# Two products of a chunk's result, issued head by head in turn over column halves, in the delta net and in the gated mixer

## The chip, the cores and the metric

The kernel runs on one core of a Trainium2 chip. The metric is the device time of one execution in microseconds (us). The engines are TensorE (PE in the profile, its weight loads PEld), VectorE (DVE), ScalarE (ACT), GpSimd (POOL) and SyncE (SP), which here only issues DMAs.

## The reference, cut to what matters

One inference step of a two-layer decoder over 512 prompt tokens and 8 samples of 4 tokens. Each layer splits one input projection among four mixers; then come an output projection, a layer norm and a channel mixer (a dense SwiGLU in the first layer, 8 experts in the second). Two of the four mixers are touched here: the gated delta net (4 heads of width 64) and HGRN2, the gated mixer (4 heads of width 64). Per chunk and head they compute:

```python
# delta net, one chunk of one head
o = einsum('ck,kv->cv', q * exp(gcum), S) + einsum('ij,jv->iv', einsum('ik,jk->ij', q, k) * decay, v_new)
S = S * exp(glast) + einsum('ck,cv->kv', k * exp(glast - gcum), v_new)
# gated mixer, one chunk of one head
o = einsum('ik,kv->iv', q * exp(b), S) + einsum('ij,jv->iv', att, v)
S = exp(blast) * S + einsum('jk,jv->kv', k * exp(blast - b), v)
```

Either result is a sum of products that go into one accumulation.

## The kernel before

The residual stream lies transposed in SBUF (features over 128 partitions, tokens along the free axis). The large products (projections, channel mixer, experts) run as three products of split operands each (`xh`, `xl` with `wh`, `wl`) on weights streamed from HBM. The small products of the mixers are float32; every float32 product is two matmul instructions in the trace, each with its own weight load.

**Work around the change.** In `mixers`, in each of the two layers, `b_chunks` works on the prompt in 4 chunks of 128 tokens with two pairs of heads, `i` = 0 and 1. A pair lies on the 128 partitions, head `h` on the half `hs(h)` (0 to 63 or 64 to 127). The chunk loop is a recurrence: the state `st` (tile `gst`) of a chunk is needed by the next. Per chunk it forms `vn` (tile `wk`), the state's new part (`kt` with `vn`), and then for each pair the result in the PSUM tile `op_` (tile `mx`): `vn` with `pt` (read from the trace as `mx<-pt,wk`) for every chunk, and from the second chunk on `st` with `q` (read as `mx<-arr,gst`), accumulated into the same columns. The first product contracts over 128 partitions into 64 result partitions (128*64 in the trace), the second over 64 into 64 (64*64), with head 0 and head 1 in opposite halves of the array's rows and of its columns. When both heads of a pair have theirs, VectorE updates the state (L1026); after both pairs ScalarE copies the result out (L1029). After the last chunk GpSimd issues the store of the state (L1030).

`mix_c` is a generator over two pairs and 4 chunks of 128 tokens. A chunk's result, in `op_` (columns 256 to 383 of `p2`, tile `mx`), is the state's product (`mx<-qec,hst`), then for each head the values `kt[:, 1]` (tile `ktc`) with `offd` and with `diag`, both 128*64. `offd` is written by ScalarE (L1197, L1200), `diag` by GpSimd. Behind them come the products for the state's update (`mx<-ktc`).

**What sets the order.** All instructions are handed to a scheduler that orders each engine's queue by a simulated timeline and fills an engine's waits with other ready work: in the trace the chunks of the delta net stand among the products of the differential attention (tiles `dx`, `pg`, `kv`), which reads its paged keys and values from HBM through SP's queue (L641), and the chunks of the gated mixer stand among its own next products (`kq`), the input projections (`st`) and the attention's last. `mm` (L292) records nearly every matmul, so groups are told apart by tiles.

Of the kernel before, what the change touches and what calls it, by code (L numbers as in the profile page):

```python
# [267 lines left out]
def _body(ctx, tc, I, O):  # L268
# [22 lines left out]
    def mm(out, lhsT, rhs, start=True, stop=True):  # L291
        return PE.matmul(out, lhsT, rhs, start=start, stop=stop)  # L292
# [192 lines left out]
    def mixers(l, y32, hook):  # L485
# [352 lines left out]
        def hs(h):  # L838
            return slice(64 * (h % 2), 64 * (h % 2) + 64)

        def b_chunks(bp, k, q, v, gt_, be, beh, kde, bge):
            def wk(w=512):
                return bp.tile([128, 512], F32, name="wk", bufs=3)[:, 0:w]
# [3 lines left out]
            kt = bp.tile([128, 2, 4, 128], F32, name="kt", bufs=1)  # L847
            erl = bp.tile([128, 2, 4], F32, name="erl", bufs=1)
            for i in range(2):
                hh = slice(2 * i, 2 * i + 2)  # L850
                for cp2 in range(2):
# [29 lines left out]
                    for u in range(2):  # L881
                        c = 2 * cp2 + u
# [111 lines left out]
            for c in range(4):  # L994
                tok = slice(128 * c, 128 * c + 128)
                vc = v[:, :, tok]
                if c > 0:
                    t1 = wk(256)
                    for h in range(2):
                        ks = mx()  # L1000
                        for i in range(2):
                            mm(ks[:, 64 * i:64 * i + 64], k[hs(h), i, tok], st[hs(h), i])
                        tt(V, t1.rearrange("p (i h d) -> p h i d", i=2, h=2)[:, h], ks[:, 0:128].rearrange("p (i d) -> p i d", i=2),
                           bc(bge[:, c].rearrange("p (i h) -> p h i", h=2)[:, h], 64), OP.mult)
                    tt(V, vc, vc, t1.rearrange("p (i d) -> p i d", i=2), OP.subtract)
                vp_ = mx()
                for i in range(2):
                    for h in range(2):
                        o = 128 * i + 64 * h
                        mm(vp_[:, o:o + 64], lt[:, 8 * i + 2 * c + h], vc[:, i, 64 * h:64 * h + 64])  # L1010
                vn = wk(256)
                S.activation(vn, vp_[:, 0:256], AF.Copy)
                op_ = mx()
                for i in range(2):
                    for h in range(2):
                        o = 128 * i + 64 * h
                        mm(op_[hs(h), 256 + 64 * i:320 + 64 * i], kt[:, i, c, 64 * h:64 * h + 64], vn[:, o:o + 64])
                for i in range(2):
                    src = op_[:, 256 + 64 * i:320 + 64 * i]
                    for h in range(2):  # L1020
                        o = 128 * i + 64 * h
                        mm(op_[hs(h), 128 * i:128 * i + 128], vn[:, o:o + 64], pt[:, 8 * i + 2 * c + h], start=True, stop=c == 0)
                        if c > 0:
                            mm(op_[hs(h), 128 * i:128 * i + 128], st[hs(h), i], q[hs(h), i, tok], start=False, stop=True)
                    if c > 0:
                        V.scalar_tensor_tensor(st[:, i], st[:, i], erl[:, i, c:c + 1], src, op0=OP.mult, op1=OP.add)  # L1026
                if c == 0:
                    V.tensor_copy(st, op_[:, 256:384].rearrange("p (i d) -> p i d", i=2))
                S.activation(v[:, :, tok], op_[:, 0:256].rearrange("p (i t) -> p i t", i=2), AF.Copy)  # L1029
# [111 lines left out]
        def mix_c(bp, sp, kk, b, q, iv):  # L1141
            oc = iv
            diag = [bp.tile([128, 2, 128], F32, name="diag%d" % a, bufs=1) for a in range(2)]
            offd = [bp.tile([128, 2, 128], F32, name="offd%d" % a, bufs=1) for a in range(2)]
# [24 lines left out]
            for i in range(2):  # L1169
                st = bp.tile([128, 128], F32, name="hst", bufs=2)  # L1170
                G.memset(st, 0.0)
                for c in range(4):
                    c0 = TOKS[c][0]
                    if c % 2 == 0:
                        kq = {s: level(s, i, c0, 256) for s in (64, 32, 16, 8, 4, 2, 1)}
                        if c:
                            yield
                    k0 = 128 * (c % 2)
                    tok = slice(c0, c0 + 128)
                    p1 = [mx() for _ in range(2)]  # L1180
                    p2 = mx()
                    for h in range(2):
                        spr = p1[h][:, 0:192].rearrange("p (g i) -> p g i", g=6)
                        mm(p1[h][0:64, 192:256], kq[64][hs(h), k0:k0 + 64], kq[64][hs(h), k0 + 64:k0 + 128])
                        for u in range(2):
                            mm(p1[h][64 * u:64 * u + 32, 256:288], kq[32][hs(h), k0 + 64 * u:k0 + 64 * u + 32],
                               kq[32][hs(h), k0 + 64 * u + 32:k0 + 64 * u + 64])
                        for j, s in enumerate((16, 8, 4, 2, 1, 0)):
                            for u in range(4):
                                sl = slice(32 * u, 32 * u + 32)  # L1190
                                ksl = slice(k0 + 32 * u, k0 + 32 * u + 32)
                                tsl = slice(c0 + 32 * u, c0 + 32 * u + 32)
                                if s:
                                    mm(spr[sl, j], kq[s][hs(h), ksl], kq[s][hs(h), ksl])
                                else:
                                    mm(spr[sl, j], kk[hs(h), i, tsl], q[hs(h), i, tsl])
                        S.activation(offd[c % 2][0:64, h, 64:128], p1[h][0:64, 192:256], AF.Copy)  # L1197
                        for u in range(2):
                            sl = slice(64 * u, 64 * u + 32)
                            S.activation(offd[c % 2][sl, h, 64 * u + 32:64 * u + 64], p1[h][sl, 256:288], AF.Copy)  # L1200
                        smx = bp.tile([128, 6, 32], F32, name="smx", bufs=2)
                        tt(V, smx, spr, C("hmask").rearrange("p (g i) -> p g i", g=6), OP.mult)
                        sml = bp.tile([128, 32], F32, name="sml", bufs=2)
                        V.tensor_reduce(sml, smx.rearrange("p g i -> p i g"), axis=AX.X, op=OP.add)
                        tt(G, diag[c % 2][:, h].rearrange("p (u i) -> p u i", u=4), mid(sml, 4), bc(C("quad"), 32), OP.mult)
                    eb = bp.tile([128, 128], F32, name="eb", bufs=2)
                    S.activation(eb, b[:, i, tok], AF.Exp)
                    kd = bp.tile([128, 128], F32, name="kdc", bufs=KDB)
                    S.activation(kd, b[:, i, tok], AF.Exp, scale=-1.0, bias=b[:, i, c0 + 127:c0 + 128])
                    tt(V, kd, kd, kk[:, i, tok], OP.mult)  # L1210
                    qe = bp.tile([128, 128], F32, name="qec", bufs=KDB)
                    tt(V, qe, q[:, i, tok], eb, OP.mult)
                    PE.transpose(p2[:, 0:128], kd, ident)
                    PE.transpose(p2[:, 128:256], iv[:, i, tok], ident)
                    kt = bp.tile([128, 2, 128], F32, name="ktc", bufs=KDB)
                    S.activation(kt, r2(p2[:, 0:256]), AF.Copy)
                    op_ = p2[:, 256:384]
                    mm(op_, st, qe, start=True, stop=False)
                    for h in range(2):
                        vs = slice(64 * h, 64 * h + 64)  # L1220
                        mm(op_[hs(h)], kt[:, 1, vs], offd[c % 2][:, h], start=False, stop=False)
                        mm(op_[hs(h)], kt[:, 1, vs], diag[c % 2][:, h], start=False, stop=True)
                    for h in range(2):
                        vs = slice(64 * h, 64 * h + 64)
                        mm(p2[hs(h), 384:448], kt[:, 0, vs], kt[:, 1, vs])
                    S.activation(oc[:, i, tok], op_, AF.Copy)
                    for h in range(2):
                        sd = st[hs(h), 64 * h:64 * h + 64]
                        V.scalar_tensor_tensor(sd, sd, eb[hs(h), 127:128], p2[hs(h), 384:448], op0=OP.mult, op1=OP.add)
                for h in range(2):  # L1230
                    G.dma_start(O["hp"][l, hs(h), i], st[hs(h), 64 * h:64 * h + 64])
                yield
# [36 lines left out]
            for i in range(2):  # L1269
                op_ = mx()  # L1270
                for h in (2 * i, 2 * i + 1):
                    mm(op_[hs(h), 0:32], vk[32 * h:32 * h + 32, 0], ats[32 * h:32 * h + 32], start=True, stop=False)
                for bb in range(NB):
                    for h in (2 * i, 2 * i + 1):
                        mm(op_[hs(h), 4 * bb:4 * bb + 4], s0[i][hs(h), bb, :], ebs[hs(h), 2, i, 4 * bb:4 * bb + 4],
                           start=False, stop=bb == NB - 1)
                V.tensor_copy(oc[:, i, sm], op_[:, 0:32])
            for i in range(2):
                sp_ = mx()
                for h2 in range(2):  # L1280
                    h = 2 * i + h2
# [918 lines left out]
```

## Time and profile before

| what | value |
|---|---|
| median of 3 timed runs | 2100.49 us (2093.48 to 2102.44) |
| profiled execution, its own time | 2082.73 us |
| its span in the trace | 2081.1 us |
| TensorE matmul busy | 1949.0 us (94%), 17620 instructions |
| VectorE busy | 1296.1 us (62%) |
| ScalarE busy | 946.4 us (45%) |
| GpSimd busy | 369.5 us (18%) |
| mean granted TensorE clock | 0.96 |

The durations come from the profiled execution. Its time lies 17.76 us under the median of the timed runs. Matmuls are pipelined and their ends are modelled, so the distance between the starts of two matmuls tells more than their durations.

### The profile page before, as it was taken

How to read it: one execution, taken by the hardware profiler on the slowest of the kernel's cores; microseconds unless marked ns; L12 is line 12 of the kernel's file. 1: busy time of each engine (PE TensorE's matmuls, PEld its weight loads, DVE VectorE, ACT ScalarE, POOL GpSimd, SP SyncE). 2: the span in 40 equal slices, each digit the busy share in tenths (PEclk: the TensorE clock that was granted, in tenths of full speed). 3: DMA queues.
4: the chain of work that ended last, by engine and by line, in shares of the span. 5: the costliest groups of instructions: out<-in, count | busy, mean ns of one | idle time of the engine just before them, and what ended most of it. 6: DMA issues, size and time to landing. Idle time of an engine off the chain costs nothing. (4 is left out here: it accounts for less than half of the span.)

```text
span 2081.1 us, 46801 instructions
## 1 busy us (share of the span) xinstructions
PE 1949.0 (94%) x17620; PEld 1755.5 (84%) x17620; DVE 1296.1 (62%) x2597; ACT 946.4 (45%) x1833; POOL 369.5 (18%) x542
## 2 busy tenths in 40 slices
PE   8999989998999999989999989995999999999985
PEld 7877747887999999978787648894999999999985
DVE  4566556766333333653566566666887877777786
ACT  3445234644322223442544234643666665556532
POOL 1220022202000000031120033100220303404350
PEclk9999998989999999999999999996999999999998
DMA  6557451332222332545554543134879868787961
GB/s 240 153 155 187 138 170 57 97 117 87 83 85 79 101 92 74 153 137 176 173 147 139 170 129 101 54 123 171 262 233 325 292 227 280 234 270 248 332 198 66
DMA packets 183924, 340.93 MB, mean 164 GB/s; under 512 B 28035, under 2 KB 103912, under 8 KB 183688
## 3 DMA queue, kind: packets, MB, share of 16 engines
q1 hardware_dynamic: 160744, 287.67, 43.4%
q0 software_dynamic: 13968, 48.04, 7.4%
q10 hardware_dynamic: 8976, 2.13, 0.5%
q8 instruction: 141, 2.31, 0.5%
q14 instruction: 95, 0.78, 0.1%
HBM read 319.91 MB, written 17.85 MB: 162 GB/s over the span
## 5 line engine op out<-in xcount | busy, mean ns | idle before, releaser
L295 DVE TENSOR_TENSOR wl<-wraw,wh 128x1024 fp32r<-128x1024 f32 (+2 forms) x474 | 550.5, 1164 | 337.0 <-ACT wh L376 331.1
L376 ACT ACTIVATE wh<-wraw 128x1024 fp32r<-128x1024 f32 (+2 forms) x474 | 463.2, 980 | 478.4 <-PE st L292 258.9
L292 PE MATMUL st<-xh,wh 128*128 128x256 f32 (+1 forms) x1536 | 461.8, 301 | 20.1 <-ACT wh L376 8.1
L292 PE MATMUL st<-xh,wl 128*128 128x256 f32 (+1 forms) x1536 | 456.8, 298 | 3.8 <-DVE wl L295 3.6
L292 PE MATMUL st<-xl,wh 128*128 128x256 f32 (+1 forms) x1536 | 456.1, 297 | 4.3 <-DVE xl L295 4.3
L292 PEld LDWEIGHTS st<-xh,wh 128*128 128x128 f32 x1536 | 299.4, 195 | 38.8 <-issue 8.8
L292 PEld LDWEIGHTS st<-xh,wl 128*128 128x128 f32 x1536 | 299.3, 195 | 16.5 <-issue 10.4
L292 PEld LDWEIGHTS st<-xl,wh 128*128 128x128 f32 x1536 | 299.6, 195 | 10.9 <-DVE xl L295 5.2
L292 PE MATMUL st<-xg,wh 128*128 128x416 f32 (+4 forms) x880 | 240.0, 353 | 2.6 <-DVE m_g L1766 1.5
L292 PE MATMUL st<-xg,wl 128*128 128x208 f32 (+4 forms) x880 | 212.4, 242 | 0.0
L292 PEld LDWEIGHTS st<-xg,wh 128*128 128x128 f32 x880 | 166.4, 189 | 4.6 <-issue 2.7
L292 PEld LDWEIGHTS st<-xg,wl 128*128 128x128 f32 x880 | 169.0, 192 | 0.0
L292 PE MATMUL st<-hg,wh 128*128 128x416 f32 (+4 forms) x440 | 123.9, 358 | 0.2 <-ACT wh L376 0.2
L1495 POOL TENSOR_SCALAR r<-r,par 128x256 f32<-128x256 f32 (+1 forms) x32 | 30.6, 969 | 449.8 <-ACT xh L1494 449.8
L292 PE MATMUL st<-hg,wl 128*128 128x208 f32 (+4 forms) x440 | 108.5, 248 | 1.9 <-DVE wl L295 1.9
L292 PE MATMUL st<-wh,xg 128*128 128x256 f32 x528 | 105.6, 293 | 4.2 <-DVE xg L1753 4.2
L295 POOL TENSOR_TENSOR m_g<-m_g,m_u 128x208 f32<-128x208 f32 (+4 forms) x55 | 52.7, 958 | 307.7 <-DVE m_u L1766 272.4
L292 PE MATMUL ff<-hh,wl 128*128 128x256 f32 (+1 forms) x352 | 101.8, 292 | 4.9 <-DVE wl L295 4.9
L292 PE MATMUL ff<-hh,wh 128*128 128x256 f32 (+1 forms) x352 | 101.8, 290 | 1.5 <-ACT wh L376 1.5
L292 PE MATMUL ff<-xh,wh 128*128 128x256 f32 (+1 forms) x352 | 102.4, 291 | 0.5 <-ACT wh L376 0.5
L292 PE MATMUL ff<-xl,wh 128*128 128x256 f32 (+1 forms) x352 | 102.2, 291 | 0.0
L292 PE MATMUL ff<-xh,wl 128*128 128x256 f32 (+1 forms) x352 | 102.0, 290 | 0.0
(583 smaller groups left out, 3851.4 us busy)
## 6 DMA issues: line engine op xcount, KB each, us to landing
pg<-in_kc_dram SPq DMA_DIRECT2D x256, 128.0 KB, 2.7
pg<-in_vc_dram SPq DMA_DIRECT2D x256, 128.0 KB, 2.5
wraw<-in_w_in_dram POOLq DMA_DIRECT2D x56, 512.0 KB, 4.4
wraw<-in_m_g_dram SPq DMA_DIRECT2D x54, 512.0 KB, 4.9
wraw<-in_m_u_dram SPq DMA_DIRECT2D x54, 512.0 KB, 4.9
wraw<-in_m_g_dram SPq DMA_DIRECT2D x65, 256.0 KB, 5.1
wraw<-in_m_u_dram SPq DMA_DIRECT2D x65, 256.0 KB, 5.7
wraw<-in_w_o_dram SPq DMA_DIRECT2D x32, 512.0 KB, 3.8
```

Of the source, the lines that this page charges most:

```text
L292: return PE.matmul(out, lhsT, rhs, start=start, stop=stop)
L295: return e.tensor_tensor(out, a, b, op=op)
L376: S.activation(h, r, AF.Copy)
L1495: G.tensor_scalar(ri[:, u], ri[:, u], gcol[:, u:u + 1], bcol[:, u:u + 1], op0=OP.mult, op1=OP.add)
```

## The change

The four products of a pair's result are issued in another order. In the delta net: `vn` with `pt` for head 0, for head 1, then `st` with `q` for head 0, for head 1 (before: both of head 0, then both of head 1). In the gated mixer: `offd` for head 0, for head 1, then `diag` for head 0, for head 1. The number of instructions, their operands, the flags that begin an accumulation and the tiles are the same; the flag that ends one stands on the last product of each head as before.

```diff
                     for h in range(2):
                         o = 128 * i + 64 * h
                         mm(op_[hs(h), 128 * i:128 * i + 128], vn[:, o:o + 64], pt[:, 8 * i + 2 * c + h], start=True, stop=c == 0)
-                        if c > 0:
+                    if c > 0:
+                        for h in range(2):
                             mm(op_[hs(h), 128 * i:128 * i + 128], st[hs(h), i], q[hs(h), i, tok], start=False, stop=True)
                     if c > 0:
                         V.scalar_tensor_tensor(st[:, i], st[:, i], erl[:, i, c:c + 1], src, op0=OP.mult, op1=OP.add)
...
                     mm(op_, st, qe, start=True, stop=False)
-                    for h in range(2):
-                        vs = slice(64 * h, 64 * h + 64)
-                        mm(op_[hs(h)], kt[:, 1, vs], offd[c % 2][:, h], start=False, stop=False)
-                        mm(op_[hs(h)], kt[:, 1, vs], diag[c % 2][:, h], start=False, stop=True)
+                    for j, a in enumerate((offd, diag)):
+                        for h in range(2):
+                            mm(op_[hs(h)], kt[:, 1, 64 * h:64 * h + 64], a[c % 2][:, h], start=False, stop=j == 1)
```

## Rows read from the trace of the kernel before

**Rows 1.** The page: busy time, then PE and its granted clock in 40 slices.
```profile
PE 1949.0 (94%) x17620; PEld 1755.5 (84%) x17620; DVE 1296.1 (62%) x2597; ACT 946.4 (45%) x1833; POOL 369.5 (18%) x542
...
PE   8999989998999999989999989995999999999985
...
PEclk9999998989999999999999999996999999999998
```

**Rows 2.** Busy time of each engine by stretch; PEclk is the mean granted clock.
```profile
core 0: us, PE busy (x) PEld busy (x) DVE busy (x) ACT busy (x) POOL busy (x), PEclk, DMA share, GB/s
240.00:440.00 200.00, 186.23 (x2250) 136.19 (x2249) 126.02 (x339) 93.25 (x255) 46.70 (x107) 0.91 0.39 113
440.00:960.00 520.00, 496.56 (x3801) 486.31 (x3801) 230.06 (x352) 171.68 (x271) 37.38 (x44) 0.99 0.35 106
```

**Rows 3.** Timeline of PE, second chunk of the delta net, first layer.
```profile
262.01 0.38 PE L292 MATMUL mx<-pt,wk 128*64 128x128 f32 x2
262.32 0.43 PE L292 MATMUL mx<-arr,gst 64*64 64x128 f32 x2
262.68 0.43 PE L292 MATMUL mx<-pt,wk 128*64 128x128 f32 x2
263.05 0.43 PE L292 MATMUL mx<-arr,gst 64*64 64x128 f32 x2
263.85 0.43 PE L292 MATMUL mx<-pt,wk 128*64 128x128 f32 x2 [0.38 <-DVE gst L1026]
264.21 0.43 PE L292 MATMUL mx<-arr,gst 64*64 64x128 f32 x2
264.57 0.43 PE L292 MATMUL mx<-pt,wk 128*64 128x128 f32 x2
264.93 0.43 PE L292 MATMUL mx<-arr,gst 64*64 64x128 f32 x2
265.29 0.44 PE L292 MATMUL mx<-gst,arr 64*128 64x64 f32 x4
```

**Rows 4.** All instructions that touch the tile gst, the state's product and its update.
```profile
L292 PE MATMUL mx<-arr,gst x48: 269/320/472, 262.3 to 1212.7; 64*64 64x128 f32 x48
L1026 DVE SCALAR_TENSOR_TENSOR gst<-gst,erl,mx x12: 279/280/282, 263.5 to 1213.1; 128x64 f32<-128x64 f32 x12
```

**Rows 5.** Timeline of PE, one array half's products in a row, one after another.
```profile
326.32 1.09 PE L292 MATMUL dx<-kv,vt 128*64 128x128 f32 x8
327.34 0.69 PE L292 MATMUL dx<-arr,y 32*128 32x512 f32 x1
```

**Rows 6.** Timeline of PE, first chunk of the delta net: no state's product.
```profile
254.50 0.61 PE L292 MATMUL mx<-pt,wk 128*64 128x128 f32 x8
255.04 0.44 PE L741 MATMUL dx<-cst,kv 128*128 128x128 f32 x2
```

**Rows 7.** Timeline of PE, the sample part of the gated mixer.
```profile
419.17 1.10 PE L292 MATMUL mx<-ebs,s2k 64*64 64x4 f32 x32
420.20 0.30 PE L292 MATMUL mx<-ats,vk 32*64 32x32 f32 x4
```

**Rows 8.** Timeline of PE, mixer chunk with nothing between its products; the last such.
```profile
360.69 0.45 PE L292 MATMUL mx<-offd,ktc 128*64 128x128 f32 x4
360.96 0.40 PE L292 MATMUL mx<-diag,ktc 128*64 128x128 f32 x4
361.18 0.29 PE L292 MATMUL mx<-ktc 128*64 128x64 f32 x4
361.40 0.39 PE L292 MATMUL st<-xh,wh 128*128 128x256 f32 x1
...
1334.13 0.45 PE L292 MATMUL mx<-offd,ktc 128*64 128x128 f32 x4
```

**Rows 9.** Timeline of PE, mixer chunk with other work between its products.
```profile
372.65 0.43 PE L292 MATMUL mx<-offd,ktc 128*64 128x128 f32 x2
373.02 0.24 PE L292 MATMUL mx<-kq 64*32 64x32 f32 x2
373.19 0.32 PE L292 MATMUL mx<-diag,ktc 128*64 128x128 f32 x1
...
373.56 0.25 PE L292 MATMUL mx<-kq 64*32 64x32 f32 x2
373.74 0.32 PE L292 MATMUL mx<-diag,ktc 128*64 128x128 f32 x1
...
374.21 0.38 PE L292 MATMUL mx<-kq 64*32 64x32 f32 x22
```

**Rows 10.** What PE waited for, 250 to 290 us: us in total, times, longest.
```profile
PE dx L292 <- DMA pg<-in_vc_dram: 0.9, 1, 0.9
```

**Rows 11.** Timeline of all engines at the end of the delta net.
```profile
288.86 0.55 POOL L1030 DMA_DIRECT2D out_gp_dram<-gst  x1 [36.40 <-DVE gst L1026]
...
295.48 0.64 PE L292 MATMUL dx<-pg,kv 128*32 128x256 f32 x8 [2.06 <-DMA pg<-in_vc_dram]
```

**Rows 12.** Busy time by stretch of 10 us, columns as in Rows 2.
```profile
260.00:270.00 10.00, 8.77 (x80) 5.00 (x80) 3.70 (x11) 3.60 (x9) 0.00 (x0) 1.00 0.40 112
...
290.00:300.00 10.00, 6.20 (x86) 3.28 (x86) 7.24 (x31) 5.83 (x18) 5.44 (x17) 1.00 0.56 166
300.00:310.00 10.00, 7.39 (x36) 2.87 (x40) 9.28 (x38) 3.38 (x9) 7.49 (x20) 0.92 0.81 238
310.00:320.00 10.00, 8.86 (x48) 6.07 (x41) 6.45 (x21) 4.74 (x13) 4.37 (x13) 0.57 0.41 122
320.00:420.00 100.00, 100.00 (x1607) 83.57 (x1608) 69.88 (x177) 57.71 (x169) 27.21 (x54) 0.95 0.27 75
```

## The prediction

> **What bounds the kernel now.** I read the page first. TensorE is busy 94% of the span and no slice of the mixers falls out of that [rows 1], so an instruction that leaves TensorE's time should be worth nearly its length, if it sits where TensorE is the last to end. The table by stretch says the same for the stage that the change touches: 186.23 of 200 us in the first layer's mixers, and 496.56 of 520 in the dense channel mixer behind them [rows 2]. Then I went to the timeline of TensorE inside one chunk. The four products of a pair of heads, two matmuls each, start 0.36 us apart (262.32, 262.68, 263.05; again from 263.85 on), small as they are [rows 3]. That spacing, and not the durations printed beside it, is the price of a product here.
>
> **Why 0.36 us.** Compare two other places. Eight matmuls of one array half and one shape, 128*64, take 327.34 - 326.32 = 1.02 us until the next shape starts [rows 5]. With p for a matmul and e for the change of shape, 8p + e = 1.02, and for a product between two changes 2p + e = 0.36 [rows 3]. So p = 0.11 and e = 0.14 us: each of the four products pays a change of shape, from 128*64 to 64*64 and back. In the first chunk, which has no state's product, four products with eight matmuls take 255.04 - 254.50 = 0.54 us [rows 6]. One after another they would take 1.02; as two column halves side by side 4p + e = 0.58. So head 0 and head 1 of the 128*64 product do run beside each other when nothing of another shape stands between.
>
> **The change, part by part: delta net.** Nothing is added or removed: the same matmuls, no DMA, no copy. The order of a pair becomes 128*64 twice, then 64*64 twice. The first two run beside each other by [rows 6]. For the second two I need a row of 64*64 products in opposite halves of rows and columns that go to one PSUM tile. The sample part of the gated mixer has it: 32 matmuls in 420.20 - 419.17 = 1.03 us, change of shape included, that is (1.03 - 0.14)/16 = 0.056 us for two of them [rows 7]. They are short (4 columns), so the row shows that both halves accept work together, and bounds nothing about 128 columns. I take the pair as side by side, 2p + e = 0.36, because the nearest row with 128 columns, [rows 6], overlaps fully; the other end, one behind the other, is 4p + e = 0.58.
>
> A pair of heads then costs 2 x 0.36 = 0.72 instead of 4 x 0.36 = 1.44 us. The very first product of a chunk comes in its own shape (262.01 to 262.32, 0.31 us) before and after, so the saving is the same. The update L1026 runs 12 times [rows 4], once for each pair of the second to fourth chunk in both layers, so there are 12 such groups (48 matmuls with the state's product are 12 x 2 heads x 2). The sum is 12 x 0.72 = 8.6 us; at the other end 12 x (1.44 - 2 x 0.58) = 12 x 0.28 = 3.4 us, if in both shapes the second product stands behind the first.
>
> The Trainium skill speaks against this edit: TensorEngine Tiling (Array Packing), section Restrictions and Gotchas, Gotcha 1, says that different row tiles cannot use one PSUM bank at once, and head 0 and head 1 of the state's product are such row tiles in one bank. By that rule the 64*64 pair would stay serial and the sum would be 12 x 0.50 = 6.0 us. The 0.056 us for two matmuls in [rows 7] do not look like it.
>
> What waits behind these products? L1026 needs both heads' products, since it overwrites the state. It now starts 0.72 us earlier, and the next pair, which stood 0.38 us for it [rows 3], follows. Head 0's state product moves behind head 1's first product, which reads a tile that is already there; no wait is added.
>
> **Gated mixer.** Both products have one shape, so there is no change of shape to save inside. Of the 16 chunks, 7 run as in the first group of [rows 8], to the last at 1334.13: four products from 360.69 to 361.18, 0.49 us, which is 4p plus little. That is already side by side, whatever order they were issued in, so the edit gives nothing there. In the other 9 other work stands between, as in [rows 9]: 374.21 - 372.65 = 1.56 us against 361.40 - 360.69 = 0.71 up to the same point; without the two visits (0.17 and 0.18) 1.21, so 0.50 us of overlap and changes of shape are lost. If all 9 lost nothing, that is 4.5 us. But what is put between stands between `offd` and `diag`, and the new order keeps that border, only with both heads on either side. I take 0.6 us, near to nothing. The other end: if the new border lets work in between the 7 whole ones, 7 x 0.50 = 3.5 us are lost. A late `offd` of head 1 would now hold up `diag` of head 0 and all that TensorE has queued behind it; the trace of the waits shows none for either tile.
>
> **What of it arrives.** 9.2 us leave TensorE. In the stretch around the delta net it is busy for 93% [rows 2], so I count 0.93 x 9.2 = 8.5 us. The rest of the stage hangs on the delta net's end too: GpSimd stands 36.40 us at the store of the state until the last L1026, with its later work behind it [rows 11], so those chains come forward with TensorE. Against the profiled execution: 2082.73 - 8.5 = 2074.2. The timed runs lie above it (median 2100.49), so I carry over the difference: 2100.5 - 8.5 = **2092 us**, 0.4% less. A measurement of this kernel tells about 0.5%, 10.5 us, from no change; the forecast falls inside that.
>
> **Rivals.**
>
> *The mixer gains too* (0.22). The 9 broken chunks close up, because the scheduler sees an independent product behind each: 8.6 + 4.5 = 13.1, times 0.93 gives 12.2 us, 2088. For it: half of the border's products now have a neighbour that is ready. Against it: where the work is put in, it was put in at the same border. The Trainium skill has a rule by which the mixer would gain otherwise: TensorE: Matmul & The Clock Gate, Part 3, says that matmuls start and end strictly in program order. Head 0's two products would then have been serial everywhere, and one slot of 0.22 us would go in each of 16 chunks, 3.5 us, so 2089. The 0.49 us of [rows 8] bear it out only if the scheduler had already put the products in the new order.
>
> *The second product stands behind the first* (0.08): 3.4 x 0.93 = 3.2 us, 2097. [rows 6] speak against it for one half of the gain, [rows 7] for the other.
>
> *The time is absorbed* (0.13). TensorE only reaches its waits for key and value pages sooner: 0.9 us at one wait before the delta net's end [rows 10], 2.06 us behind it [rows 11], and 290 to 320 us holds 7.6 us of idle time [rows 12]. If pages come no earlier, 4.3 us per layer vanish there: 2100, no change. Against it: SP's page loads wait for TensorE to free their buffers, so they move forward with it, and from 320 to 420 us TensorE is busy all of 100 us [rows 12].
>
> *Slower: idle TensorE drops its clock* (0.07). Where TensorE idled, at 290 to 310 us (13.59 of 20 us busy), the next 10 us were granted 0.57 of the clock, close to 1.2 GHz [rows 12]; at that level a 10 us stretch does the work of 5.7. If shorter chunks put more idle time there and the low level lasts longer, each 10 us cost 4.3. From 20 us more in the two layers together the gain is gone, from 44 us on the kernel is slower by over 0.5%; with 60 us more, 26 - 8.5 = 17.5 us, 2118. Against it: 260 to 270 us was also idle for 1.2 us and stayed at 1.00 [rows 12].
>
> **Chances and range.** The forecast has 0.50. Its own terms run from 6 us (one shape serial) to 11 us, so a part of it, about 0.13, lies beyond 10.5 us; of the mixer's rival at 12.2 about 0.19. Faster by over 0.5%: 0.32. Slower: 0.07 and a little for an order of the scheduler that costs in the mixer (3.5 us) and elsewhere, 0.08. Within: 0.60. The range reaches to 2083 (the mixer's rival, less the 4.5 us by which the timed runs spread) and to 2103 (time absorbed, plus 2 to 3 us of that spread); below lies some 0.1, above some 0.1.
>
> **What will show it.** In the profile after, in each of 12 groups: `pt` of both heads starting within some hundredths of a us, `gst` of both heads 0.36 us later, the next instruction another 0.36 us later. If the `gst` pair takes 0.58, one shape is serial. In the mixer: four `offd` matmuls together, four `diag`, and nothing or one visit between. If the groups shrink and the span does not, the waits for `pg` between 290 and 330 us must have grown. The prediction is wrong if the scheduler lays the stage out anew, which would show in the order of the work around these groups, not in them.

## The result, and the profile after

| | before | after |
|---|---|---|
| median | 2093.48 us (2082.57 to 2110.67, 20 runs) | 2076.74 us (2069.26 to 2088.54, 20 runs) |
| ratio | | 0.9927, 95% interval [0.9910, 0.9945] |
| profiled execution | 2082.73 us | 2087.53 us |

The kernel is faster by 0.73%, 15.3 us (11.5 to 18.8). The median of before is lower here than the 2100.49 us of its first three runs, which are among these twenty and lie from their middle upwards. The two profiled executions mislead if they are set side by side: that of before is one of the fastest of its kernel, that of after one of the slowest of its own. So these two spans are not compared below, but groups of instructions and stages, over several kernels.

The page of after, which answers to [rows 1] (busy time; PE and its granted clock in 40 slices): TensorE is as busy as before and nearly the whole of the span.

```profile
PE 1947.4 (93%) x17620; PEld 1754.9 (84%) x17620; DVE 1296.5 (62%) x2597; ACT 947.4 (45%) x1833; POOL 366.9 (18%) x542
...
PE   8999989998999999989999979995999999999985
...
PEclk9999988999999999999999999996999999999998
```

The timeline of TensorE in the delta net of after, at full clock, answers to [rows 3]. A row is a run of equal instructions; the first number is the start.

```profile
281.24 0.39 PE L292 MATMUL mx<-pt,wk 128*64 128x128 f32 x4
281.56 0.44 PE L292 MATMUL mx<-arr,gst 64*64 64x128 f32 x4
281.92 0.91 PE L292 MATMUL dx<-arr,y 32*128 32x384 f32 x2
...
283.83 0.44 PE L292 MATMUL mx<-pt,wk 128*64 128x128 f32 x4
284.20 0.44 PE L292 MATMUL mx<-arr,gst 64*64 64x128 f32 x4
284.56 0.44 PE L292 MATMUL mx<-gst,arr 64*128 64x64 f32 x4
```

Both heads' `pt` products now make one row of four matmuls, and 0.37 us later come both heads' state products; the next shape starts another 0.36 us on. A pair costs 284.56 - 283.83 = 0.73 us, where the four rows of [rows 3] took 1.44. The other pair of heads takes 281.92 - 281.24 = 0.68, instead of 1.40 before.

A whole and a broken chunk of the gated mixer in after answer to [rows 8] and [rows 9]:

```profile
365.48 0.44 PE L292 MATMUL mx<-offd,ktc 128*64 128x128 f32 x4
365.75 0.39 PE L292 MATMUL mx<-diag,ktc 128*64 128x128 f32 x4
365.97 0.28 PE L292 MATMUL mx<-ktc 128*64 128x64 f32 x4
...
377.44 0.44 PE L292 MATMUL mx<-offd,ktc 128*64 128x128 f32 x4
377.71 0.38 PE L292 MATMUL mx<-diag,ktc 128*64 128x128 f32 x2
378.02 0.25 PE L292 MATMUL mx<-kq 64*32 64x32 f32 x4
378.21 0.32 PE L292 MATMUL mx<-diag,ktc 128*64 128x128 f32 x1
```

The whole chunk takes 0.49 us from `offd` to `ktc`, as before. The broken ones stay nine; this one has a visit of other work less. The nine together, from the first `offd` to behind the last `diag` and without the visits, took 7.5 us before and 6.9 after.

### The profile page after: what moved, and what is told of

The parts are those of the page before. It is cut to its first block, busy times and chain, and to the rows that moved or that the text cites. A ratio compares the mean times of both kernels' runs of the same rounds, so it can differ in the third digit from the quotient of the medians.

```text
span 2085.8 us, 46807 instructions
## 1 busy us (share of the span) xinstructions
PE 1947.4 (93%) x17620; PEld 1754.9 (84%) x17620; DVE 1296.5 (62%) x2597; ACT 947.4 (45%) x1833; POOL 366.9 (18%) x542
## 5 line engine op out<-in xcount | busy, mean ns | idle before, releaser
L292 PE MATMUL ff<-hl,wh 128*128 128x256 f32 (+1 forms) x352 | 101.7, 290 | 0.0
```

## The experiments

Each kernel ran beside the kernel before on one chip; differences in us are the ratio's distance from 1 times the 2095 us of before. "Sum of the groups" is, from the timeline of TensorE, the time from the first to behind the last result product of each of the 12 groups, waits left out.

### Each half alone, and the groups eight times

`dn_only` has the delta net's half of the diff, `mix_only` the mixer's. `old8` and `new8` issue the delta net's result products eight times from the second chunk on, in the old and in the new order; the repeats write the same result over it again, so this is added work.

```diff
+                    for _ in range(8 if c > 0 else 1):
                         for h in range(2):
                             ...
```

> Only the delta net has the new order; the gated mixer has the old one. Theory 1 (TensorE's time in the groups is what counts): the 12 groups give 8.6 us, so 8 to 9 us less than the kernel before. Theory 2 (the mixer's groups and the order that the scheduler lays around them give the rest of the 15 us): also 8 to 9 us, and what is missing to 15 is in the run with the mixer alone. Theory 3 (a us taken out of the chunk recurrence is worth more than a us, because the work behind it starts sooner and TensorE's clock stays up): 13 to 16 us less.

> Only the gated mixer has the new order; the delta net has the old one. Theory 1: 0.6 us less, not to be told from no change. Theory 2: 4 to 7 us less. Theory 3: 0.6 us, as theory 1.

> The result's products of the delta net are issued 8 times over from the second chunk on, in the old order (the repeats overwrite each other, the result is the same); the mixer is old. By the spacing of 0.36 us each group costs 7 x 1.44 = 10.1 us more, 12 groups 121 us: about 2093 + 121 = 2214 us under every theory, a little less where repeats fall into idle time. Its use is the difference to the next run.

> As the run before, but each of the 8 repeats in the new order. Theories 1 and 2: a group of 8 costs 8 x 0.72 less, 12 groups 69 us, so 64 to 69 us under the run with the old order. Theory 3 (each us is worth about 1.7): 110 to 120 us under it.

Measured: `dn_only` 0.9953 [0.9930, 0.9976], 9.8 us less; `mix_only` 1.0010 [0.9984, 1.0036]. So the delta net carries the gain; the two halves alone sum to 7.7 us, not to 15.3. `old8` took 1.0613 [1.0571, 1.0655] and `new8` 1.0201 [1.0166, 1.0236]: 86 us apart (some 11 to either side), more than 8 times 8.6. By the profile the delta net of layer 0 is 34.9 us shorter in `new8` (8 x 6 x 0.72 = 34.6: the groups, within 0.3 us) and that of layer 1 by 55.7. What is too much in layer 1 goes with its clock, at least in the profiled execution, which of `old8` is the slowest of its six. Busy time by stretch (the two numbers ahead of the last two are the granted clock and the DMA share) of `old8`, and below it its timeline there:

```profile
1240.00:1260.00 20.00, 18.44 (x112) 11.43 (x110) 5.83 (x14) 5.47 (x13) 0.53 (x1) 0.77 0.26 79
1260.00:1280.00 20.00, 20.00 (x80) 9.22 (x79) 0.28 (x1) 0.49 (x1) 0.00 (x0) 0.50 0.19 53
1280.00:1300.00 20.00, 20.00 (x70) 9.42 (x68) 3.18 (x9) 0.81 (x2) 0.00 (x0) 0.50 0.13 37
```

```profile
1282.68 0.69 PE L292 MATMUL mx<-pt,wk 128*64 128x128 f32 x2
1283.30 0.69 PE L292 MATMUL mx<-arr,gst 64*64 64x128 f32 x2
1283.92 0.69 PE L292 MATMUL mx<-pt,wk 128*64 128x128 f32 x2
```

and `new8` at the same place of its own:

```profile
1220.00:1240.00 20.00, 20.00 (x192) 10.41 (x192) 4.95 (x14) 3.12 (x8) 0.00 (x0) 0.92 0.46 137
```

From 1260 us on TensorE is busy for all of 40 us and runs at 1.2 GHz; a product costs 0.62 us there instead of 0.36. A TensorE that the page calls 100% busy can be at its lower level.

### The same kernels again, and an exchange that makes nothing cheaper

`after_again` and `before_again` are copies. `sham` keeps the old order with the heads exchanged, `for h in (1, 0)`, in both places of the diff.

> The changed kernel once more, for more runs and a second profile. Theory 1 (TensorE's time in the groups at full clock is all): 9.2 us less in the trace, ratio 0.9956, so the first measurement (0.9927) was at the far end of its error and this one lies nearer to 0.995. Theory 2 (the scheduler's new order around the layer's mixers gives the rest): 0.993 again. Theory 4 (the old order also costs more whenever TensorE is granted its lower clock, 2.47 instead of 1.44 us a group, and the profile of before happened to be of its fastest run): 0.9935 to 0.9945, and low clock in some groups of this profile.

> The kernel before against itself: ratio 1.000 within its interval. Its profile is a second look at an ordinary run: theory 4 wants several of the 12 groups at the lower clock (0.62 us from one product to the next instead of 0.36), theories 1 and 2 say nothing of it.

> The old order with head 1 before head 0 in both places: the same changes of shape, the same overlap, but the scheduler lays the mixers and the experts out anew. Theories 1 and 4: ratio 1.000. Theory 2: anything up to 6 us either way, as the layout falls.

Measured: `after_again` 0.9934 [0.9912, 0.9955], 13.8 us less; `before_again` 0.9990 [0.9968, 1.0011]. The result repeats. `sham` 0.9950 [0.9928, 0.9972], 10.5 us less: its groups sum to 19.1 us, no cheaper than before's 17.4 to 17.6, so a kernel can gain more than the whole forecast here without the change. No theory of the first set had foreseen that.

### A filler for the tail of layer 0

In the trace of before the stretch behind layer 0's last mixer chunk runs partly at the lower level, and in after less of it does. From the store of the mixer's state to one fixed `st` matmul of the output projection (its 313th) it takes 58.8 us in before and 55.3 in after, with TensorE's queue in the same order. The two tables by stretch, `before_again` first, `after` second:

```profile
421.70:431.70 10.00, 9.85 (x109) 6.82 (x108) 5.85 (x15) 3.66 (x7) 2.19 (x4) 0.75 0.22 69
431.70:441.70 10.00, 7.36 (x29) 6.00 (x30) 5.55 (x10) 5.05 (x11) 0.00 (x0) 0.67 0.11 41
441.70:451.70 10.00, 9.49 (x62) 9.20 (x62) 5.61 (x10) 3.09 (x3) 0.00 (x0) 0.73 0.44 118
```

```profile
420.60:430.60 10.00, 9.85 (x112) 7.09 (x111) 5.85 (x15) 4.44 (x8) 2.19 (x4) 0.83 0.28 94
430.60:440.60 10.00, 7.33 (x32) 6.21 (x31) 6.94 (x12) 5.14 (x10) 0.00 (x0) 0.66 0.07 20
440.60:450.60 10.00, 10.00 (x86) 10.00 (x85) 6.81 (x11) 3.18 (x3) 0.00 (x0) 1.00 0.61 193
```

`warm_before` and `warm_after` add matmuls there whose results nobody reads; `sham_dn` exchanges the heads in the delta net only, `sham_new` has the new order with them exchanged in both places.

```diff
             for i in range(2):
+                if l == 0:
+                    mm(mx(), C("bones"), big.rearrange("p b v -> p (b v)"))
                 op_ = mx()
...
             rms_gate(oc, i, P("norm_c")[:, l:l + 1], gg[0][:, i])
+            if l == 0:
+                wt = mx()
+                for _ in range(2):
+                    mm(wt, C("bones"), oc[:, i, 0:512])
```

> The old order, with six products of 512 columns added in layer 0 behind the last mixer chunk (one ahead of each 32-matmul row of the mixer's samples, two behind each of the two last gates, 0.73 us each by the row of eight 32*64 matmuls in the trace, 4.4 us in all), where TensorE stood idle at 428.1 and 431.3 us and ran at the lower of its two levels. Their results are read by nobody. Theory A (8 us of the change's gain lie in the groups, 4 to 5 us in the clock of this tail, which in the old kernel happens to be low for some 20 us): the granted clock of the tail rises to 0.9 or more, its 58.8 us become about 56 to 57 although work was added, and the time is 0 to 3 us below the kernel before. Theory B (the low clock there costs nothing that the end sees): 3 to 4.4 us above the kernel before. Theory C (the filler doesn't hold the clock): the clock of the tail stays at 0.67 to 0.75 and the time rises by 4 to 6 us.

> The new order with the same six added products; the order of TensorE's queue is else that of the kernel after. Theory A: its tail (55 us) gets 0 to 2 us longer, and it lies 7 to 11 us under the old order with the same filler, the sum that was counted in the groups (8.6 us forecast, 7.4 to 8.3 in the traces), instead of the 15 us that were measured without filler. Theory B: the distance stays at 14 to 15 us. Theory C: the distance stays and both are 4 to 6 us longer.

> The new order with head 1 ahead of head 0 in both places; no group gets cheaper or dearer than in the kernel after. The old order with the heads exchanged had gained 10.5 us although its groups cost 19.1 us, as in the kernel before. If the groups' gain stands by itself: 7 to 9 us under that kernel, 17 to 19 us under the kernel before (ratio 0.991 to 0.992). If exchanging the heads and the new order find the same 5 to 10 us elsewhere and once only, about as far as the kernel after (ratio 0.993) and no more than 4 us under the exchanged old order.

> The old order with head 1 ahead of head 0 in the delta net only. No group gets cheaper: their sum stays at 17 to 19 us. Theory A: the time follows the tail of layer 0: 4 to 5 us less than before where that tail is at 54 to 55 us, no change where it is at 58 to 59. A theory by which any exchange of heads gains: 10 us less, whatever the tail.

Measured: `warm_before` 1.0027 [1.0005, 1.0049], `warm_after` 1.0013 [0.9987, 1.0038]; 3 us apart, with intervals that hold both 0 and 9. The filler was badly placed. It waits for the gate's last product and the output projection waits for it, as the timeline of `warm_before` shows:

```profile
430.38 3.65 PE L292 MATMUL mx<-y,cst 128*128 128x512 f32 x4 [2.97 <-DVE y L295]
...
437.90 1.96 PE L292 MATMUL mx<-y,cst 128*128 128x512 f32 x4 [2.25 <-DVE y L295]
```

The tail grew to 61.7 and 63.1 us though its last 288 `st` matmuls ran at full clock (39.3 us instead of 41.0): the test is inconclusive, and both kernels are no faster than before. `sham_dn` has one of the shortest tails (54.1 us) and a time of 0.9988 [0.9959, 1.0017]; that speaks against theory A, but the interval holds the 4 to 5 us that it asks for. The next runs say more: `vp_old` and `vp_new` have tails of 55.7 and 55.5 us and lie 12.6 us apart, so the tail does not carry that difference. `sham_new` 0.9943 [0.9915, 0.9971], 11.9 us less, and only 1.5 us below `sham`.

### The same exchange at another place, under the old and the new order

`vp_old`, `vp_new`: `for h in (1, 0)` at the product that forms `vn`; `kn_old`, `kn_new`: at `kt` with `vn`. (The percentages that the third expectation gives for the two earlier exchanges are not theirs; they are 0.50 and 0.12%, for 10.5 and 2.5 us.)

> The old order; only the two heads of the product that forms vn are exchanged, and the order of kinds on TensorE's queue is that of the kernel before. If the spread between kernels comes from where the rest falls, this one, whose queue is that of the kernel before, gives no change, within 3 us. If an exchange of heads gains by itself: 5 to 10 us less.

> The new order with the same exchange at vn; the order of kinds on TensorE's queue is that of the kernel after. If the 15 us belong to the new order with its queue as it stands: 13 to 17 us under the kernel before. If only the groups' sum is the order's own and the rest is chance of the run: 7 to 10 us.

> The old order; the two heads of the product that forms the state's new part are exchanged, and the scheduler lays out a small part of the delta net's stage anew. Placement alone: anything from no change to 10 us less, as the two exchanges before (1.2 and 0.5%, 10.5 and 2.5 us). No group gets cheaper: sum 17 to 19 us.

> The new order with the exchange at the state's new part. If the order's own gain is the groups' sum: 7 to 10 us under the old order with the same exchange. If the order and the exchange find the same gain once: under 4 us.

Measured: `vp_old` 1.0004 [0.9980, 1.0028] and `vp_new` 0.9944 [0.9920, 0.9967], 12.6 us apart. `kn_old` 0.9978 [0.9954, 1.0003] and `kn_new` 0.9976 [0.9948, 1.0005]: no difference that this can tell.

How far the rest of TensorE's queue stays the same can be read from the traces, matmul by matmul, without the products of the diff and those with tile `t`, which start within some ns of each other. Between before and `before_again` 2 stand at another place, between before and `vp_old` and between after and `vp_new` as few. Between before and after, and so in the `vp` pair, it is some 140, of which 125 in layer 1's mixer (1240 to 1290 us of before); in the `sham` pair some 250, in the `kn` pair 5, and 3 between before and `mix_only`. The new order is thus worth about 13 us where a new layout of layer 1's mixer comes with it (`vp`), 1.5 us in `sham`, whose pair differs most, and 0.4 us in `kn`, the pair that changes the products of the diff and hardly anything else. Each of these has some 7 to 8 us to either side, so the groups' 8.6 us lie at the very edge of what `kn` allows.

**All profiles together** (us; from starts in the traces; the fillers' left out). "L0" and "L1" run from the delta net's first result product to the store of the last mixer chunk's state in that layer; "tail" is the stretch above; "rest" is the span without these three.

```
                groups     L0     L1   tail    rest    span   ratio timed
before            17.6  163.7  163.5   58.8  1695.0  2081.1   1
before_again      17.4  165.3  165.7   58.8  1703.5  2093.3   0.9990
vp_old            17.4  161.4  165.5   55.7  1707.7  2090.3   1.0004
mix_only          19.4  166.6  168.9   57.2  1704.8  2097.6   1.0010
sham_dn           17.1  165.0  165.9   54.1  1705.8  2090.9   0.9988
kn_old            17.7  163.1  166.3   54.3  1706.0  2089.7   0.9978
sham              19.1  171.5  158.1   53.6  1708.0  2091.2   0.9950
mean, old order   17.9  165.2  164.9   56.1  1704.4  2090.6
kn_new             9.1  162.7  163.9   54.3  1702.0  2082.9   0.9976
dn_only           10.3  164.9  157.5   54.0  1704.9  2081.3   0.9953
sham_new           8.6  159.6  158.1   55.2  1709.7  2082.5   0.9943
vp_new             9.1  160.1  160.7   55.5  1704.5  2080.9   0.9944
after_again        9.1  160.3  160.5   54.6  1704.2  2079.5   0.9934
after             10.1  163.6  160.4   55.3  1706.5  2085.8   0.9927
mean, new order    9.4  161.9  160.2   54.8  1705.3  2082.2
```

The groups are 8.5 us cheaper in the new order, and the two stages L0 and L1 together 8.0 us shorter (330.1 to 322.0; they scatter by 3 us within either order, so give or take 3.6). Tail and rest differ by 1.3 and 0.9 us, less than they scatter. So by the profiles what is freed in the groups arrives in the stages and at the end, on the mean. Part of what L1 gains goes with the clock: its length times what its granted clock lacks to 1 is 15.1 us in the old order and 11.1 in the new, on the mean. What single kernels gain beyond the groups, by the timed runs, differs by layout.

**Where the layout's part may lie.** The mean granted clock of the timed runs is 0.9607, 0.9608 and 0.9605 in `after`, `after_again` and `vp_new`, the three whose queue is that of after; every other set has 0.954 to 0.959, before 0.957. Within the sets 0.001 of clock goes with 1.5 us, so 0.004 goes with 6 us: about what these three gain beyond the groups. The clock does not rank the others, though: `sham_new` has the lowest, 0.9543, and gains 11.9 us. One place was found where the traces differ. Some 50 us behind layer 1's delta net, in the mixer, TensorE's clock falls, and it stays low for some 14 us in `before_again`, `vp_old`, `kn_old`, `sham_dn`, `mix_only` and `kn_new`, 7 us in `before`, `sham`, `dn_only` and `sham_new`, and 3 us in `after`, `after_again` and `vp_new`. By stretch, `before_again`, then `kn_new`, then `after_again`:

```profile
1266.00:1276.00 10.00, 10.00 (x199) 6.63 (x198) 6.61 (x17) 5.51 (x19) 2.36 (x5) 0.84 0.33 107
1276.00:1286.00 10.00, 10.00 (x91) 7.81 (x91) 5.75 (x18) 4.55 (x15) 3.85 (x8) 0.50 0.16 55
```

```profile
1265.00:1275.00 10.00, 10.00 (x119) 7.68 (x110) 6.72 (x19) 5.46 (x18) 4.09 (x9) 0.50 0.17 52
```

```profile
1256.00:1266.00 10.00, 10.00 (x153) 7.29 (x153) 6.73 (x15) 4.54 (x15) 2.16 (x4) 0.84 0.33 107
1266.00:1276.00 10.00, 10.00 (x162) 8.03 (x162) 7.12 (x22) 5.88 (x20) 3.69 (x8) 0.96 0.17 54
```

All these stretches are 100% busy; at 0.50 they hold 91 matmuls, at 0.96 162. In the timeline the same input projection shows both levels. `before_again`:

```profile
1276.00 0.41 PE L292 MATMUL st<-xh,wh 128*128 128x256 f32 x1
1276.21 0.41 PE L292 MATMUL st<-xl,wh 128*128 128x256 f32 x1
1276.43 0.41 PE L292 MATMUL st<-xh,wl 128*128 128x256 f32 x1
```

`after_again`, where the level comes back in the middle of it:

```profile
1266.41 0.41 PE L292 MATMUL st<-xh,wl 128*128 128x256 f32 x1
1266.63 0.34 PE L292 MATMUL st<-xh,wh 128*128 128x256 f32 x1
1266.81 0.28 PE L292 MATMUL st<-xl,wh 128*128 128x256 f32 x1
1266.93 0.28 PE L292 MATMUL st<-xh,wl 128*128 128x256 f32 x1
```

The starts lie 0.21 us apart at the lower level and 0.12 at the full one. Ten us at half the clock cost 5. That the length of this stretch sets the layout's part is only argued, from one profile of each kernel and the clocks of the timed runs; no run lengthened or shortened the stretch alone. Two things in the same profiles speak against it. Before, with the queue of `before_again`, shows 7 us and not 14. And the stretch lies inside L1: with the groups it should make L0 and L1 together some 13 us shorter in the three kernels with after's queue, but they sum to 321.9 us, against 330.1 in the four with the queue of before (`before`, `before_again`, `vp_old`, `mix_only`), 8.2 us and no more than the groups. So the part beyond the groups is seen in the timed runs alone.

## Why the prediction was off

**The price of a product and the group: right.** 1.44 us became 0.73 (forecast 0.72), with `pt` of both heads starting 7 ns apart and so with `gst`; 12 groups: 17.9 to 9.4 us over all profiles, 8.5 against 8.6. The row that the forecast took for the 64*64 pair had only 4 columns; with 128 they overlap as well.

**The rule that spoke against it: not borne out.** The two state products of a pair, one behind the other, would have taken 0.58 us; they took 0.36 to 0.37 us in after at full clock. By the Trainium skill, TensorEngine Tiling (Array Packing), section Restrictions and Gotchas, Gotcha 1, different row tiles cannot use one PSUM bank at once. The trace does not agree.

**The mixer: right in size.** 0.6 us in the nine broken chunks (forecast 0.6), nothing in the seven whole ones, and `mix_only` at 1.0010. The rival that the mixer gains too fell with it. The reason given was not quite right: the work put in between did not keep to one border between `offd` and `diag`; in [rows 9] it parts the two products of either head, and in after it stands between the `diag` of the two heads (377.71 to 378.21). The rival's other version fell as well: the whole chunks take 0.49 us in either order, and the queue of before was not in the new order already, since in the chunk of [rows 9] a `diag` starts at 373.19 us ahead of an `offd` at 373.20. That version rested on the Trainium skill, TensorE: Matmul & The Clock Gate, Part 3, by which matmuls start and end in program order. Nothing of the 3.5 us that it would have given was seen.

**The rival of absorption: a part of it, most in layer 1.** Waits for pages from the delta net's first result product to the mixer's store in layer 1, `before_again` first, `after` second (engine, what it waited for: us in total, times, longest):

```profile
PE dx L292 <- DMA pg<-in_kc_dram: 2.5, 3, 1.4
PE dx L292 <- DMA pg<-in_vc_dram: 0.7, 1, 0.7
```

```profile
PE dx L292 <- DMA pg<-in_kc_dram: 6.3, 9, 1.6
PE dx L292 <- DMA pg<-in_vc_dram: 0.6, 1, 0.6
```

On the mean of the seven old-order and the six new-order profiles they sum to 3.1 and 5.6 us in layer 1, and over the same stage of layer 0 to 4.1 and 5.1. TensorE does reach its pages sooner. Some waits for VectorE fell, and all of TensorE's idle time grew by 1.0 us in layer 0 and 1.2 in layer 1. Layer 0 gained 3.3 us and layer 1 4.7, half of 8.5 each being freed; in layer 1 some 4 us less were lost to the lower clock, so its gain is not that of the groups alone.

**What of it arrives: the step that failed.** "9.2 us leave TensorE ... so I count 0.93 x 9.2 = 8.5 us", and from there 2092 with a foot at 2083. Over the thirteen profiles the 8.5 us are nearly what arrives (8.0). But the measured kernel got 13.8 to 15.3, and so did `vp_new` nearly (11.7), with TensorE's clock 0.004 higher in the timed runs. What failed is that the sum has no term for a new layout: 5 to 7 us on the fast side that were put at nothing. The forecast's own sign of it came true, since some 140 other matmuls stand elsewhere in after, most of them in layer 1's mixer. Of the clock the forecast knew only a rival on the slow side, at 0.07; it went the other way, and by the slope above about 6 us go with it. `sham` shows that such a term needs no change of price at all: 10.5 us from exchanging the heads. A range for this kernel must reach 5 to 10 us to either side for layout alone.

**The base: too high.** The forecast carried its 8.5 us to the median of three runs, 2100.49; the twenty runs beside the result give 2093.48. With that base the same working gives 2085, and the measured 2076.74 would still lie 8 us under it; the foot of the range, 2083, would come to 2076. So two errors, 7 us of base and 5 to 7 of layout, put the result outside the range; either alone would have left it inside, near 2085.

**What stays open.** Where the 5 to 7 us beyond the groups come from; why the clock's low stretch in layer 1's mixer is 3 us long behind one layout and up to 14 behind others; and how much of the result the new order owns for good. The stages say 8.0 us, give or take 3.6, with some of the clock in it. By timed ratios the three new orders with another queue than after's (`dn_only`, `sham_new`, `kn_new`) average 0.9957 and the three old ones with another queue than before's (`sham_dn`, `kn_old`, `sham`) 0.9972, 3 us apart; the two kernels as they stand, 14 to 15.

## What to carry to other kernels

Where products of two array shapes alternate, issue all of one shape before the next: here two products then worked side by side in opposite halves for the price of one, 0.36 us, and the starts of matmuls in the trace gave that price in advance. Before a gain of under one per cent is put down to an edit, measure an edit that makes nothing cheaper, and compare the order of the queue around the edit: here an exchange of heads moved the time by 10.5 us in one of four places (in the other three by what can't be told from nothing), and the edit itself moved some 140 other matmuls.

## What the runs showed of the hardware that was not expected

TensorE ran at 1.2 GHz for 40 us while 100% busy, in `old8` from 1260 to 1300 us, where the products shown alternate between two shapes; in the 20 us before it had been busy for 18.44. The low stretches of layer 1's mixer also begin and last while it is 100% busy. Two fp32 products of 64 rows and 128 columns in opposite quarters of the array, into one PSUM tile, took 0.36 us, as long as one between two changes of shape.
